# The transposes at the end of RWKV's pairs: from TensorE to 32x32 blocks that go by way of DRAM

## The chip, the core and the metric

The kernel runs on one core of a Trainium2 chip. The metric is the device time of one launch in microseconds (us). The core has five engines that run their own instruction streams in order and wait for each other through semaphores: PE (TensorE, matmuls; its weight loads are listed as PEld), DVE (VectorE), ACT (ScalarE), POOL (GpSimd) and SP (SyncE, which in this kernel issues nearly all DMAs). PE writes its results to PSUM banks; DVE and ACT take them from there.

## What is computed

One layer of a streaming encoder on 512 frames with 2048 channels, all float32. One input projection feeds two groups of heads, RWKV-7 (16 heads of 64 channels) and HGRN2 (8 heads of 128); their gated outputs go through one output projection, and a residual with LayerNorm ends the layer:

```
proj = x @ w_in
rw   = y + shift_mu * (y_prev - y)            # RWKV's columns: y is proj, y_prev one frame before
# RWKV-7, for each head, frame by frame:
S = S * w_t + (S @ a_t) b_t^T + v_t k_t^T;  o_t = S @ r_t
o = (o - mean) * rsqrt(var + GN_EPS) * gn_w + gn_b        # over the head's 64 channels
o_rwkv = (o + sum(r * k * r_k) * v) * silu(z)
o_hgrn = rms_norm(hgrn2(q, f, i)) * g_norm_w * silu(z_h)
out = layer_norm(ALPHA * x + concat(o_rwkv, o_hgrn) @ w_out) * ln_w + ln_b
```

The change is in the lines that begin with `o =` and `o_rwkv =`.

## The kernel before, in words

**Matmuls.** The projections run in a split form: each float32 operand is divided into a high part (rounded to the type `fp32r`) and a low part (the rest), and three matmuls add up high x high, high x low and low x high. All of them are issued in `three` (line 453). The input projection works through units of 128 columns, 16 k-tiles of 128 channels each; the order of the units (`_order`) is, for each group of two pairs of RWKV heads, k, r, v of both pairs, the z of the group before, then the HGRN columns. The last two units are z of pairs 6 and 7. The weights of a unit come in parts of 128x512; ACT writes the high part `wh` (line 337, called from `split`) and DVE the low part `wl` (line 347). `wh` and `wl` have three buffers each, and a part is asked for two parts ahead of its use. Weight loads (`wr`, line 430) are DMAs of 512 KB for two parts.

**RWKV.** Two heads make a pair (128 channels); there are 8 pairs in 4 groups of two. `rwkv_prep` forms the scan's operands and turns some of them by 32x32 blocks: `turned` has DVE transpose each 32x32 block of a tile (line 366), then 8 or 16 small DMAs on SP (line 401) bring the blocks to their places. `rwkv_group` inverts the triangular matrices, runs the scan over 8 chunks of 64 frames and adds the outputs. Up to here o has frames on the partitions: tile `S["o"]` is a view of `S["ot"]`, [128 frames, 4 blocks of frames, 128 channels].

**The end of a pair**, `rwkv_finish`: with frames on the partitions, it takes mean and variance over each head's 64 channels (DVE reductions, an ACT square, a power -0.5 on POOL) and scales o. Then o must have channels on the partitions, because z, the bonus `S["bv"]`, the weights gn_w and gn_b, and the output projection have them there. Four transposes on PE (line 328, the helper `tr`) bring it to a PSUM bank, and DVE gates it from there into tile `g`. All ends go through one queue, `finishes`: the end of pair 7 begins when that of pair 6 is done.

**The order of the work** is not found by hand. A planner (`Plan`) runs while the program is built, with a clock for each engine, a cost for each operation (`tt`, `stt`, `act`, `dtr`, `mm` and so on) and a due time for each tile (`plan.ready`, when it is there to be read; `plan.busy`, when its place may be written). The projections' matmuls are the main line; after each one `pump` goes through the queues of side threads in a fixed order (splits, evacuations, scans, groups, finishes, preps, heads, stores), and a thread's next operation is issued when by the plan's clocks its operands are nearly there: for DVE and ACT within 0.5 to 0.6 us of now, for PE 0.35 us after. A thread may also yield a condition (`room(...)`: so many free tiles of a kind; `by_now(t)`: t is there by the plan; `landed(...)`: the same and a free PSUM bank of the kind `mix`). The planner sets only the order of instructions in each engine's stream; on the chip they wait for semaphores.

**The output projection** has four blocks of 512 columns. The first (`rows` with d=0) takes the 16 gated tiles in the order 0 to 5, 8 to 13, 14, 6, 15, 7; 0 to 7 are RWKV's pairs, 8 to 15 HGRN's heads. At the start of k-tile j it calls `ahead`, which loads spilled tiles again and splits the gated tile j+1 into `xh` (ACT) and `xl` (DVE). At j = 8 it also asks for the LayerNorm's weights, `ln_wb`, one DMA of 2 MB on SP (line 1473). The tiles of all pairs but 6 and 7, and of all heads but the last two, are written to DRAM (`spill`) when they are done and read again here.

## Time and profile before

| | |
|---|---|
| time, median of 3 runs | 1050.75 us (1050.46 to 1051.28) |
| the profiled execution | 1050.24 us, of which the profile's span is 1048.5 |
| granted TensorE clock | 0.999 |
| PE busy | 1040.6 us, 99% of the span |
| DVE, ACT, POOL busy | 755.7, 437.6, 38.3 us |
| DMA | 114.79 MB in 87305 packets; SP's queue is busy for 36.6% of 16 engines' span |
| transposes on PE (line 328) | 88 of 128x128, of which 32 are RWKV's ends and 56 HGRN's |

Each timeline row has the start, the duration, the engine, the line, the operation with what it writes and reads, and in brackets the idle time before it with what ended it. Durations of matmuls overlap, so their price is read from start to start. A group's row gives busy time, the mean of one in ns, and the idle time before. The chain of waits is followed back from the last instruction; its pieces are a start, a length and what ran.

### The profile page before, as it was taken

The numbers are of one execution on the slowest core, as the hardware profiler recorded it, in microseconds if no ns is written. First come the engines' busy times: TensorE is split into PE (matmuls) and PEld (weight loads), VectorE is DVE, ScalarE is ACT, GpSimd is POOL, SyncE is SP. The second block draws the span as 40 slices with busy tenths as digits, with TensorE's granted clock in tenths as the row PEclk, the third lists the DMA queues.
The fourth block names the chain that finished last, engine by engine and source line by source line (L and its number), as shares of the span: only waits on it lengthen the run. The fifth ranks groups of instructions, "written<-read, shape, count | busy, mean of one in ns | idle before, by whom it ended". The sixth has DMA issues, their size and how long they took to land.

```text
span 1048.5 us, 18840 instructions
## 1 busy us (share of the span) xinstructions
PE 1040.6 (99%) x7342; PEld 865.1 (83%) x7342; DVE 755.7 (72%) x1653; ACT 437.6 (42%) x867; POOL 38.3 (4%) x81
## 2 busy tenths in 40 slices
PE   9999999999999999999999999999999999999997
PEld 8888888888888888888888888888888888888885
DVE  7465898667759987676689866865998778625556
ACT  6545333445353354452533353525334554323321
POOL 0000000000000000000000000000000002000000
PEclk9999999999999999999999999999999999999999
DMA  8134342222343522223534323234352244545613
GB/s 332 54 103 114 99 109 86 86 79 81 84 123 100 122 82 74 78 98 79 138 78 118 98 62 96 70 96 110 100 128 72 69 164 131 182 131 159 202 60 131
DMA packets 87305, 114.79 MB, mean 109 GB/s; under 512 B 56368, under 2 KB 58160, under 8 KB 87088
## 3 DMA queue, kind: packets, MB, share of 16 engines
q1 hardware_dynamic: 87072, 113.39, 36.6%
q8 instruction: 58, 0.95, 0.4%
q14 instruction: 31, 0.25, 0.1%
q10 hardware_dynamic: 144, 0.20, 0.1%
HBM read 99.92 MB, written 7.34 MB: 102 GB/s over the span
## 4 chain that ended last, share of the span: by engine, by line
PE 99%; DVE 1%; DVEq 0%; issue 0%
PE main L453 74%; PE mix L324 11%; PE mix L453 8%; PE main L1192 3%; PE main L324 2%; PE mix L328 1%; PE mix L1142 0%; DVE inv L356 0%; DVE inv L347 0%; DVE stats L1549 0%; DVEq L1663 0%; DVE mv L1357 0%; DVE bd L356 0%; DVE mv L352 0%; DVE inv L1140 0%
## 5 line engine op out<-in xcount | busy, mean ns | idle before, releaser
L453 PE MATMUL main<-xl,wh 128*128 128x512 f32 x864 | 341.1, 395 | 0.0
L453 PE MATMUL main<-xh,wl 128*128 128x512 f32 x864 | 341.1, 395 | 0.0
L453 PE MATMUL main<-xh,wh 128*128 128x512 f32 x864 | 340.9, 395 | 0.0
L337 ACT ACTIVATE wh<-wr 128x512 fp32r<-128x512 f32 x299 | 186.9, 627 | 237.1 <-PE main L453 180.5
L347 DVE TENSOR_TENSOR wl<-wr,wh 128x512 fp32r<-128x512 f32 x299 | 203.8, 682 | 61.8 <-ACT wh L337 60.1
L453 PEld LDWEIGHTS main<-xh,wh 128*128 128x128 f32 x864 | 162.4, 188 | 33.0
L453 PEld LDWEIGHTS main<-xh,wl 128*128 128x128 f32 x864 | 162.5, 188 | 32.6
L453 PEld LDWEIGHTS main<-xl,wh 128*128 128x128 f32 x864 | 162.4, 188 | 32.6
L453 PE MATMUL main<-wl,xh 128*128 128x512 f32 (+1 forms) x262 | 102.6, 392 | 0.0
L453 PE MATMUL main<-wh,xh 128*128 128x512 f32 (+1 forms) x262 | 102.1, 390 | 0.0
L453 PE MATMUL main<-wh,xl 128*128 128x512 f32 (+1 forms) x262 | 101.6, 388 | 0.0
L453 PEld LDWEIGHTS main<-wh,xh 128*128 128x128 f32 x262 | 49.2, 188 | 9.9
L453 PEld LDWEIGHTS main<-wh,xl 128*128 128x128 f32 x262 | 49.2, 188 | 9.7
L453 PEld LDWEIGHTS main<-wl,xh 128*128 128x128 f32 x262 | 49.2, 188 | 9.6
L338 ACT ACTIVATE t<-main,om 128x512 f32<-128x512 f32 x33 | 22.4, 687 | 51.1 <-PE main L453 41.6
L356 DVE SCALAR_TENSOR_TENSOR t<-main,pr,t 128x511 f32<-128x511 f32 x33 | 24.4, 747 | 26.5 <-ACT t L338 26.2
L347 DVE TENSOR_TENSOR inv<-inv,inv 64x30 f32<-64x30 f32 (+14 forms) x120 | 38.6, 322 | 2.9
L347 DVE TENSOR_TENSOR inv<-inv 64x30 f32<-64x30 f32 (+14 forms) x120 | 38.4, 320 | 2.3
L347 DVE TENSOR_TENSOR t<-t,tot 128x256 f32<-128x256 f32 x96 | 37.8, 414 | 1.8 <-PE mix L324 1.7
L356 DVE SCALAR_TENSOR_TENSOR bd<-mix,pc,bd 64x64 f32<-64x64 f32 x112 | 31.7, 283 | 7.5 <-PE mix L324 5.2
L337 ACT ACTIVATE zz<-mix 64x64 f32<-64x64 f32 x63 | 13.8, 220 | 46.9 <-PE mix L324 45.8
L338 ACT ACTIVATE t<-main 128x512 f32<-128x512 f32 x32 | 18.5, 598 | 30.7 <-PE main L453 30.2
(222 smaller groups left out, 1328.0 us busy)
## 6 DMA issues: line engine op xcount, KB each, us to landing
wr<-w_all SPq DMA_DIRECT2D x156, 512.0 KB, 3.6
q<-head SPq DMA_DIRECT2D x15, 448.0 KB, 5.9
q<-q SPq DMA_DIRECT2D x128, 32.0 KB, 2.4
g<-x_r SPq DMA_DIRECT2D x16, 256.0 KB, 3.8
spill<-g SPq DMA_DIRECT2D x12, 256.0 KB, 2.7
out<-q SPq DMA_DIRECT2D x12, 256.0 KB, 2.4
t<-spill SPq DMA_DIRECT2D x10, 256.0 KB, 4.2
zz<-ksq SPq DMA_DIRECT2D x64, 32.0 KB, 2.6
```

Of the source, the lines that this page charges most:

```text
L324: return Op([("pe", cost, lambda: pe.matmul(o, l, r, start=start, stop=stop, **kw))], [l, r], [o], mode="narrow" if narrow else "main" if ...
L328: return Op([("pe", 0.11, lambda: pe.transpose(o, i, ident))], [i], [o])
L337: return "act", cost, lambda: sc_e.activation(o, i, f, scale=scale)
L338: return "act", cost, lambda: sc_e.activation(o, i, f, scale=scale, bias=bias)
L347: return dve_op([a, b], o, lambda: dve.tensor_tensor(o, a, b, f), base=0.16 if o.shape[0] < P and size(o) == C and o.tensor.name in tags e ...
L356: return dve_op([a, b], o, lambda: dve.scalar_tensor_tensor(o, a, s, b, f1, f2), per=0.00113, base=0.085 if o.shape[0] == P else 0.25 if s ...
L453: pe.matmul(ps, l, r, start=first and i == 0, stop=last and i == 2)
L1192: pe.matmul(pss[a], *ops, start=k == 0 and low == of == 0, stop=k == KT - 1 and low == 1)
```

## The change

The four PE transposes of a pair's end are replaced by a way through DVE and DRAM. `turned_far` has DVE transpose the 32x32 blocks of o into tile `g`, used here as a temporary. One DMA writes it to a tile `far` in DRAM (256 KB, rows of 2 KB); after 4.4 us of the plan's PE clock, four DMAs read it back with the blocks in exchanged places (64 KB each, in pieces of 512 bytes) into `S["ot"]`, the tile that o was in. It is due 4.7 us later. ACT then applies the scale gn_w and the shift gn_b (both halved, as before) and puts the frames in order on the way into `g`; DVE adds `bv` and multiplies by z's gate. Before, two operations of DVE did this, the first out of PSUM. A `ksq` tile for the gate is now taken after the turn, not before.

The two pairs of a group get a queue each, so their ends run beside each other. And `turned` now marks its temporary tile as busy until its DMAs have landed by the plan.

```diff
@@ turned, and new functions
-        plan.ready[name] = (plan.clock["pe"] + 3.0, "dma")
+        plan.ready[name] = plan.busy[tmp.tensor.name] = (plan.clock["pe"] + 3.0, "dma")
+
+    def turned_far(dst, src, tmp):
+        yield dtr(tmp, src.rearrange("p c (b f) -> p b c f", f=32))
+        yield lambda: by_now(tmp)
+        far = dpool.tile([4, 32, 4, T // 4], F32, tag=nm("far"), name=nm("far"))
+        nc.sync.dma_start(far.rearrange("a p b r -> (a p) b r"), tmp.rearrange("p b c f -> p b (c f)"))
+        at = plan.clock["pe"] + 4.4
+        yield lambda: plan.clock["pe"] >= at
+        for b in range(4):
+            nc.sync.dma_start(dst[32 * b : 32 * b + 32].rearrange("p a c f -> p a (c f)"),
+                              far[:, :, b].rearrange("a p r -> p a r"))
+        plan.ready[dst.tensor.name] = plan.busy[dst.tensor.name] = (plan.clock["pe"] + 4.7, "dma")
+
+    def in_blocks(t):
+        return t.rearrange("p (c a f) -> p c a f", a=4, f=32)
+
+    def blocks(t):
+        return t.rearrange("p (a c f) -> p a c f", c=4, f=32)
@@ rwkv_finish
         yield has(S, "z", "bv")
-        yield room(g=1, ksq=1)
+        yield room(g=1)
         g = take("g")
+        yield from turned_far(blocks(S["ot"]), o_all, blocks(g))
+        yield room(ksq=1)
         sz = take("ksq")
         z = S["z"]
-        yield landed(o_all)
-        po = take("mix")
-        for j in range(4):
-            yield tr(po[:, j * P : j * P + P], o_all[:, j])
         yield act(sz, z, AF.Tanh, scale=0.5)
-        yield stt(g, po, hcol(HGW, p), S["bv"], ALU.mult, ALU.add)
-        drop(po)
+        yield act(in_blocks(g), blocks(S["ot"]).rearrange("p a c f -> p c a f"), AF.Identity,
+                  scale=hcol(HGW, p), bias=hcol(HGB, p))
         yield stt(z, sz, 1.0, z, ALU.add, ALU.mult)
-        yield stt(g, g, hcol(HGB, p), z, ALU.add, ALU.mult)
+        yield tt(g, g, S["bv"], ALU.add)
+        yield tt(g, g, z)
@@ rwkv_group
-                plan.add(finishes, rwkv_finish(S, 2 * grp + i))
+                plan.add(finishes[i], rwkv_finish(S, 2 * grp + i))
@@ queues
-    groups, finishes, preps = plan.queue(), plan.queue(), plan.queue()
+    groups, finishes, preps = plan.queue(), [plan.queue(), plan.queue()], plan.queue()
```

## The prediction

> **What bounds the kernel now.** I read the page first: busy shares, then the chain that ended last.

> ```profile
> span 1048.5 us, 18840 instructions
> PE 1040.6 (99%) x7342; PEld 865.1 (83%) x7342; DVE 755.7 (72%) x1653; ACT 437.6 (42%) x867; POOL 38.3 (4%) x81
> ...
> PE 99%; DVE 1%; DVEq 0%; issue 0%
> ```

> TensorE is never without work for long. Its own waits, the whole list:

> ```profile
> PE mix L324 <- ACT ksq L1409: 1.5, 1, 1.5
> PE mix L1142 <- DVE inv L1140: 1.1, 1, 1.1
> PE mix L324 <- DVE bd L356: 0.4, 1, 0.4
> ```

> These are 3.0 us in all, so each microsecond of PE work taken out shortens the run, and each new PE wait lengthens it. The place to look is the junction at the end: the ends of pairs 6 and 7 run beside the first column block of the output projection, which consumes `gated[6]` as its 14th and `gated[7]` as its 16th k-tile. The chain there, from 868 to 910 us, and the PE timeline around pair 7's transposes:

> ```profile
> 880.39 0.44 PE mix L328 x4
> 880.83 7.99 PE main L453 x35
> 888.82 0.44 PE mix L328 x4
> 889.25 4.12 PE main L453 x18
> 893.37 0.44 PE mix L328 x4
> 893.81 13.43 PE main L453 x59
> ```

> ```profile
> 892.98 0.39 PE L453 MATMUL main<-wh,xh 128*128 128x512 f32 x1
> 893.21 0.60 PE L328 MATMUL mix<-cst,t 128*128 128x128 f32 x4
> 893.56 0.48 PE L453 MATMUL main<-wl,xh 128*128 128x512 f32 x1
> 893.88 0.40 PE L453 MATMUL main<-wh,xl 128*128 128x512 f32 x1
> ```

> A plain matmul takes 13.43/59 = 0.228 us. From 892.98 to 893.88 two of them pass, 0.455 us; 0.90 are used, so four transposes with both turns cost 0.445 us, as the chain's 0.44 says. The sets at 880.39 and 893.37 are pairs 6 and 7; 888.82 is an HGRN head and stays. The 60 matmuls from 893.56 to 907.2 are five k-tiles of 12, so I number the block's k-tiles 0 to 15: tile 11 starts at 893.56 and a tile is 2.73 us.

> **The change: what is gained.** Eight pairs give up four transposes each: 8 x 0.445 = 3.6 us of PE, 0.34% of the run. Nothing else of PE changes, and a `mix` bank is free earlier, which no PE wait above asks for.

> [...]

> **What is added on DVE and ACT.** The nearest rows, by group:

> ```profile
> L366 DVE STREAM_TRANSPOSE ksq<-t 128x512 f32<-128x512 f32 x8 | 5.6, 701 | 0.0
> L356 DVE SCALAR_TENSOR_TENSOR g<-mix,half,t 128x512 f32<-128x512 f32 x16 | 12.0, 747 | 9.0 <-PE mix L328 8.8
> L356 DVE SCALAR_TENSOR_TENSOR g<-g,half,t 128x512 f32<-128x512 f32 x8 | 6.0, 746 | 0.1
> L347 DVE TENSOR_TENSOR t<-t,sm 128x512 f32<-128x512 f32 x16 | 11.1, 692 | 4.7 <-POOL sm L379 4.4
> L338 ACT ACTIVATE t<-main,om 128x512 f32<-128x512 f32 x33 | 22.4, 687 | 51.1 <-PE main L453 41.6 <-PE main L1192 8.6 <-DVE xl L347 0.8
> ```

> Per pair DVE gains a block transpose (0.70) and two tensor_tensors (1.38) and loses two scalar_tensor_tensors (1.49): +0.6 us, 4.7 us over eight pairs on an engine with 293 us free. ACT gains one scaled pass, 0.69 us, 5.5 in all with 611 free. Both hide under PE as throughput; if not, they would cost at most 10.2 us, and I take nothing, because splits run two parts ahead of PE. The same ACT row shows projections evacuated as soon as PE ends them (41.6 of 51.1 us idle are waits for PE): the `t` tiles that pairs now hold some 10 us longer have room in groups 0 to 2, and no one there needs `gated` before the spill. There I cost the longer chain at nothing; a shortage could cost up to those 10 us, a lucky order gain 1. Marking `tmp` busy until its DMAs land moves only planned starts: 0, within 1 us either way.

> **DMAs.** Each pair issues one 256 KB write and four 64 KB reads on SP: 40 issues, 4 MB. The prices:

> ```profile
> spill<-g SPq DMA_DIRECT2D x12, 256.0 KB, 2.7
> ...
> zz<-ksq SPq DMA_DIRECT2D x64, 32.0 KB, 2.6
> ...
> big<-ln_wb SPq DMA_DIRECT2D x1, 2048.0 KB, 10.1
> ```

> A write of 2.7 fits in the 4.4 us left for it, and reads near 2.6 (four issues: some 4) in the 4.7. So the plan's path is 0.7 + 0.6 + 4.4 + 4.7 = 10.4 us up to ACT, against about 1 us now. In groups 0 to 2 it holds. At the junction it meets the last row: 2 MB of `ln_wb`.

> **The junction, step by step** (times of before; the 24 earlier transposes move everything alike). DVE, POOL and SP there:

> ```profile
> 878.83 0.69 DVE L347 TENSOR_TENSOR t<-t,sm 128x512 f32<-128x512 f32 x1
> ...
> 884.59 0.68 DVE L360 TENSOR_REDUCE sm<-t 128x8 f32<-128x512 f32 x1
> ```

> ```profile
> 877.15 1.64 POOL L379 TENSOR_TENSOR sm<-sm,mhalf 128x8 f32<-128x8 f32 x1 [9.47 <-DVE sm L353]
> ```

> ```profile
> 885.13 1.26 SPq L1473 DMA_DIRECT2D big<-ln_wb  x1
> 890.09 0.33 SPq L430 DMA_DIRECT2D wr<-w_all  x1
> ```

> Pair 6's last norm multiply ends at 879.5. Pair 7 waits for its turn until 884.59 now; with its own thread it starts with pair 6, on a DVE already nearly full there. That can move pair 6 by -0.6 to +1.2 (one foreign instruction ahead, or two); I take +0.5: 880.0. POOL does the second power behind the first, so pair 7 is ready some 1.6 to 2 us later, 881.8. Pair 6: block transpose to 880.7, write at 881.4 (the planner lets about 0.6 pass, as between 879.5 and PE's transposes), reads in SP's order at 885.8. `ln_wb` is asked for at the start of tile 8, now 885.13 - 0.45 = 884.7, **ahead of them**. Does a later DMA overtake it? The next weight load was issued at 890.09; ACT's timeline:

> ```profile
> 890.50 0.63 ACT L337 ACTIVATE wh<-wr 128x512 fp32r<-128x512 f32 x1 [1.60 <-PE main L453]
> 891.04 0.62 ACT L337 ACTIVATE xh<-g 128x512 fp32r<-128x512 f32 x1
> ...
> 893.18 0.63 ACT L337 ACTIVATE wh<-wr 128x512 fp32r<-128x512 f32 x1 [1.00 <-PE main L453]
> 893.72 0.61 ACT L337 ACTIVATE xh<-g 128x512 fp32r<-128x512 f32 x1
> 896.54 0.63 ACT L337 ACTIVATE wh<-wr 128x512 fp32r<-128x512 f32 x1 [2.21 <-DMA wr<-w_all]
> ```

> It landed at about 896.4, 6.3 us after its issue and 1.2 after `ln_wb` (885.13 + 10.1 = 895.2): it queued. [...]

> So pair 6's reads land 0.6 (half the load's bytes) to 1.2 us (small packets) after 894.8: 895.4 to 896.0, where the plan has 890.5; pair 7's 0.6 to 1.2 later. The new ACT pass stands in ACT's order from about 890.0 of the plan, pair 7's from about 891.8, and ACT is in order: behind it queue the weight split of tile 12 (now at 890.50), the gated split of tile 12 (891.04), and on DVE the low halves, behind the pair's two tensor_tensors. Released at 895.7, ACT does the pass (0.55 at its rate), then the splits: 896.9 and 897.4, DVE's low halves at 898.2 and 898.8. PE's tile 12 is due at 893.56 + 2.73 - 0.89 = 895.4 and can run its third matmul from 898.8, so it starts 2.9 us late. If pair 7's pass is ahead of the splits too, 3.9. If tile 11's split (due one tile earlier) is caught, tile 11 waits from 892.7 to 897.1: 4.4. Bounds 2.9 to 4.4, and I take the middle, 3.6. After that PE runs a tile late, and `gated[6]` (about 897.7) and `gated[7]` come in time.

> **Sum.** On the profiled execution (1050.24 us, span 1048.5 and 1.7 around it): -3.6 + 3.6 = 0, 1050.2. The median of the runs is 0.5 above it: 1050.7; own range 1050.0 to 1051.6.

> **Rivals.** *The wait is escaped.* If both passes come into ACT's order behind tile 12's splits (plan time past 892.7, 2.7 us later than I think), only tile 13's `gated[6]` is late: pass 896.3, tensor_tensors 897.6, splits 898.9 and 899.5 against a need at 898.1: 1.0 us, hence 1050.7 - 3.6 + 1.0 = 1048.1. If the reads get ahead of `ln_wb` (both norms 1 to 3 us earlier) nothing waits: 1047.1. For: 1 us on pair 6 decides, planned orders shift by that. Against: two threads on one DVE and one POOL make it later, and pair 7 needs it as well.

> *Pair 7's write is caught too*, the slower side: if its norm ends after 884.7 - 0.6 - 0.7 = 883.4, the write queues behind `ln_wb`, SP holds the reads (and weight loads behind them) until about 896, they land 2.6 later at 898.6, pass 899.2, two tensor_tensors, splits done at 901.6: tile 12 runs from 901.2, 5.8 late: 1050.7 - 3.6 + 5.8 = 1052.9. For: POOL's row, 1.64 us a piece, and DVE's load. Against: my 881.8 leaves 1.6 us.

> **Chances.** This kernel's measurement tells 0.2%, 2.1 us, from no change: faster is under 1048.65, slower over 1052.85. The forecast 0.53, escape 0.30, the second trip 0.17. Range 1047.0 (nothing waits) to 1053.3 (the second trip with tile 11 caught), less than 2 in 10 outside.

> **What would show it.** The 32 RWKV transposes gone and PE busy down by 3.6; `ln_wb` ahead of the last reads on SP; reads there landing after 8 us or more, elsewhere under 4.7; an ACT idle of 5 us ending in a DMA of the pair's tile near 895; a PE wait of 3 to 4 us on ACT or DVE splits. No PE wait there and 1047 would make the forecast wrong; so would waits of PE in groups 0 to 2.

## The result, and the profile after

The changed kernel takes 1067.59 us (median of 4 runs, 1066.48 to 1069.47) against 1050.61 for the one before, timed beside it: a ratio of 1.0163, 95% interval 1.0145 to 1.0181. The prediction was 1050.7 with a range of 1047.0 to 1053.3, so the time lies far outside of it.

The page of the changed kernel (its lines are those of the new file: `three` is now line 474, weight loads are 451, the turned blocks' small DMAs still 401, the write to `far` 413, the four reads 417):

```profile
span 1065.8 us, 18884 instructions
PE 1044.9 (98%) x7310; PEld 866.0 (81%) x7310; DVE 757.8 (71%) x1660; ACT 442.6 (42%) x876; POOL 38.6 (4%) x81
...
PE 90%; SPq 3%; DMA 2%; DVE 2%; issue 1%; ACT 1%; DVEq 0%; ACTq 0%
```

PE has 32 instructions less, as it should. But it is busy 4.3 us longer, and idle 1065.8 - 1044.9 = 20.9 us against 7.9. The chain of waits, 99% PE before, is 90% PE now; most of the rest is SP's queue, DMAs and DVE. PE's own waits in the changed kernel (total, times, longest):

```profile
PE main L474 <- ACT xh L337: 4.5, 2, 3.9
PE mix L324 <- ACT ksq L337: 3.6, 2, 2.1
PE mix L324 <- DVE ksq L347: 2.9, 3, 1.0
PE mix L324 <- DVE uph L347: 1.9, 1, 1.9
```

Two more, of 1.5 and 1.1 us, are at the ends of the run and were there before; one of 0.6 us has no releaser. The first row here is at the last junction (912 to 921 us), which the prediction had looked at. The other three are 8.4 us in groups 0 to 2 (near 298, 516 to 524 and 727 us), where it had expected nothing.

**Group 0, step by step.** SP's timeline of the changed kernel (start, length of the issues, what):

```profile
279.74 5.16 SPq L401 DMA_DIRECT2D q<-q  x8
285.00 0.54 SPq L413 DMA_DIRECT2D far<-g  x1
285.59 2.56 SPq L401 DMA_DIRECT2D q<-q  x4
288.25 0.54 SPq L451 DMA_DIRECT2D wr<-w_all  x1
288.83 3.29 SPq L401 DMA_DIRECT2D q<-q  x4
292.22 1.97 SPq L417 DMA_DIRECT2D t<-far  x4
```

DVE had the blocks turned at 280.7 (its row starts at 280.02 and takes 0.71), but SP was busy with `turned`'s small DMAs of the next group's preparation, 0.64 us an issue, and wrote `far` only at 285.0. Another eight of them and a weight load stand between the write and the reads. The reads go out from 292.2 to 294.2. Now ACT, and then PE:

```profile
295.78 0.81 ACT L338 ACTIVATE g<-t,half 128x512 f32<-128x512 f32 x1 [7.27 <-DMA t<-far]
296.50 0.61 ACT L337 ACTIVATE wh<-wr 128x512 fp32r<-128x512 f32 x1
297.02 0.61 ACT L337 ACTIVATE ksq<-t 128x512 fp32r<-128x512 f32 x1
```

```profile
297.69 0.50 PE L324 MATMUL mix<-ksq,ones_r 128*128 128x512 f32 x1 [2.14 <-ACT ksq L337]
299.18 0.51 PE L324 MATMUL mix<-ksq,ones_r 128*128 128x512 f32 x1 [0.99 <-DVE ksq L347]
...
300.22 0.63 PE L474 MATMUL main<-xh,wl 128*128 128x512 f32 x1
300.65 0.63 PE L474 MATMUL main<-xh,wh 128*128 128x512 f32 x1
...
303.41 0.40 PE L474 MATMUL main<-xl,wh 128*128 128x512 f32 x1
303.65 0.40 PE L474 MATMUL main<-xh,wl 128*128 128x512 f32 x1
```

ACT stands 7.27 us at the new pass, with a weight split and the operand `ksq` of another thread behind it. PE then waits for that `ksq`, 2.14 us, and for its low half from DVE, 0.99. After the wait PE's matmuls follow each other every 0.43 us, not 0.23 (300.22 to 300.65 against 303.41 to 303.65), for 3.4 us; the profile gives the granted clock as 0.50 there and 1.00 before and after. So waits of 3.13 us are followed by a loss of an estimated 1.7 us (half of 3.4), about half as much again. In groups 1 and 2 ACT stands at the same pass, 5.00 us (until 512.79) and 6.80 us (until 725.15).

**The last junction.** SP again:

```profile
895.21 0.38 SPq L1493 DMA_DIRECT2D big<-ln_wb  x1
895.65 0.42 SPq L413 DMA_DIRECT2D far<-g  x1
900.27 0.33 SPq L451 DMA_DIRECT2D wr<-w_all  x1
905.39 1.98 SPq L417 DMA_DIRECT2D t<-far  x4
907.42 0.52 SPq L413 DMA_DIRECT2D far<-g  x1
```

Pair 6's write, not only its reads, is behind `ln_wb`; SP can issue the reads only when it has landed, 9.7 us later, and pair 7's write stands behind those reads. ACT reaches the pass at 901.3, runs it at 909.13, and PE waits 3.91 us at 912.64:

```profile
909.13 0.81 ACT L338 ACTIVATE g<-t,half 128x512 f32<-128x512 f32 x1 [7.85 <-DMA t<-far]
```

```profile
912.64 0.79 PE L474 MATMUL main<-wh,xh 128*128 128x512 f32 x1 [3.91 <-ACT xh L337]
```

### The profile page after: what moved, and what is told of

Same layout as the page of the kernel before. It is cut to its first block, busy times and chain, and to the rows that moved or that the text cites. A ratio compares the mean times of both kernels' runs of the same rounds, so it can differ in the third digit from the quotient of the medians.

```text
span 1065.8 us, 18884 instructions
## 1 busy us (share of the span) xinstructions
PE 1044.9 (98%) x7310; PEld 866.0 (81%) x7310; DVE 757.8 (71%) x1660; ACT 442.6 (42%) x876; POOL 38.6 (4%) x81
## 4 chain that ended last, share of the span: by engine, by line
PE 90%; SPq 3%; DMA 2%; DVE 2%; issue 1%; ACT 1%; DVEq 0%; ACTq 0%
PE main L474 66%; PE mix L324 10%; PE mix L474 8%; PE main L1212 3%; SPq L401 2%; PE main L324 2%; DMA far<-g 1%; DMA t<-far 1%; PE mix L328 1%; DMA zz<-ksq 1%; SPq L417 1%; DVE g L347 0%; DVE wl L347 0%; PE mix L1162 0%; ACT g L338 0%
## 5 line engine op out<-in xcount | busy, mean ns | idle before, releaser
L337 ACT ACTIVATE wh<-wr 128x512 fp32r<-128x512 f32 x299 | 185.8, 626 | 220.4 <-PE main L474 150.4
L347 DVE TENSOR_TENSOR wl<-wr,wh 128x512 fp32r<-128x512 f32 x299 | 203.5, 682 | 74.2 <-ACT wh L337 73.0
L338 ACT ACTIVATE t<-main,om 128x512 f32<-128x512 f32 x33 | 22.3, 685 | 50.9 <-PE main L474 41.6
L356 DVE SCALAR_TENSOR_TENSOR t<-main,pr,t 128x511 f32<-128x511 f32 x33 | 24.4, 746 | 24.8 <-ACT t L338 24.8
L347 DVE TENSOR_TENSOR inv<-inv,inv 64x30 f32<-64x30 f32 (+14 forms) x120 | 38.5, 321 | 2.5
L347 DVE TENSOR_TENSOR inv<-inv 64x30 f32<-64x30 f32 (+14 forms) x120 | 38.4, 320 | 2.4
L356 DVE SCALAR_TENSOR_TENSOR bd<-mix,pc,bd 64x64 f32<-64x64 f32 x112 | 31.7, 283 | 11.5 <-PE mix L324 9.3
L347 DVE TENSOR_TENSOR t<-t,tot 128x256 f32<-128x256 f32 x96 | 37.5, 415 | 2.0 <-PE mix L324 1.5
L338 ACT ACTIVATE t<-main 128x512 f32<-128x512 f32 x32 | 18.5, 595 | 33.4 <-PE main L474 33.2
L337 ACT ACTIVATE zz<-mix 64x64 f32<-64x64 f32 x64 | 14.0, 219 | 40.2 <-PE mix L324 39.6
## 6 DMA issues: line engine op xcount, KB each, us to landing
g<-x_r SPq DMA_DIRECT2D x16, 256.0 KB, 4.2
spill<-g SPq DMA_DIRECT2D x12, 256.0 KB, 2.1
out<-q SPq DMA_DIRECT2D x12, 256.0 KB, 2.4
t<-spill SPq DMA_DIRECT2D x10, 256.0 KB, 4.1
```

The costliest lines, as they stand in the source:

```text
L337: return "act", cost, lambda: sc_e.activation(o, i, f, scale=scale)
L338: return "act", cost, lambda: sc_e.activation(o, i, f, scale=scale, bias=bias)
L347: return dve_op([a, b], o, lambda: dve.tensor_tensor(o, a, b, f), base=0.16 if o.shape[0] < P and size(o) == C and o.tensor.name in tags e ...
L356: return dve_op([a, b], o, lambda: dve.scalar_tensor_tensor(o, a, s, b, f1, f2), per=0.00113, base=0.085 if o.shape[0] == P else 0.25 if s ...
```

## The experiments

All ratios are to the kernel before, timed on the same chip beside each run.

| run | edit | median us | ratio (95%) |
|---|---|---|---|
| after | the change | 1067.59 | 1.0163 (1.0145 to 1.0181) |
| e1 | threads and busy mark alone | 1051.23 | 1.0006 (0.9997 to 1.0016) |
| e2 | due after 12.0 | 1058.46 | 1.0078 (1.0063 to 1.0093) |
| e3 | `ln_wb` in block 2 | 1068.35 | 1.0171 (1.0136 to 1.0206) |
| e4 | e2 + e3 | 1059.32 | 1.0086 (1.0069 to 1.0102) |
| e5 | DMAs on ACT's queue | 1054.03 | 1.0031 (1.0020 to 1.0042) |
| e6 | e2 + gate's tile late | 1053.72 | 1.0033 (1.0020 to 1.0047) |
| e7 | e6, pairs 6 and 7 on PE | 1048.99 | 0.9986 (0.9976 to 0.9995) |
| e8 | e5 + gate's tile late | 1060.76 | 1.0096 (1.0080 to 1.0113) |
| e9 | after, pairs 6 and 7 on PE | 1059.12 | 1.0081 (1.0066 to 1.0096) |
| e10 | e6 + `ln_wb` in block 2 | 1051.95 | 1.0014 (1.0005 to 1.0023) |
| e11 | e8 + `ln_wb` in block 2 | 1061.31 | 1.0097 (1.0082 to 1.0112) |
| e12 | e8 + e9 | 1050.74 | 1.0002 (0.9992 to 1.0011) |
| e13 | e6 + `ln_wb` at k-tile 14 | 1049.39 | 0.9987 (0.9978 to 0.9996) |

### The small edits alone (e1)

The kernel before, with a queue for each pair's end and with `plan.busy[tmp]`; the transposes stay on PE.

```diff
-        plan.ready[name] = (plan.clock["pe"] + 3.0, "dma")
+        plan.ready[name] = plan.busy[tmp.tensor.name] = (plan.clock["pe"] + 3.0, "dma")
-                plan.add(finishes, rwkv_finish(S, 2 * grp + i))
+                plan.add(finishes[i], rwkv_finish(S, 2 * grp + i))
```

> The kernel before with only the two small edits: a queue for each pair's end, and the temporary tile of the turned blocks marked busy until its DMAs land. The transposes stay on TensorE. Theory A (the loss comes from ACT passes that stand in ACT's order before their data can have landed): 1049 to 1052 us, no PE waits beyond the 3.0 us of before, since no pass waits for a DMA. Theory B (the new order of the ends, or the busy mark, crowds DVE and ACT and by itself makes PE wait): 1056 us or more, with PE waits for DVE or ACT at the groups' ends.

1051.23 us against 1050.67 beside it, no change that can be told. PE's waits, complete:

```profile
PE mix L324 <- ACT ksq L1409: 1.5, 1, 1.5
PE mix L1142 <- DVE inv L1140: 1.1, 1, 1.1
PE mix L324 <- DVE t L347: 0.2, 1, 0.2
```

By themselves the threads and the mark cost nothing that can be told; theory B falls.

### The due time (e2), ln_wb (e3), and both (e4)

```diff
-        plan.ready[dst.tensor.name] = plan.busy[dst.tensor.name] = (plan.clock["pe"] + 4.7, "dma")
+        plan.ready[dst.tensor.name] = plan.busy[dst.tensor.name] = (plan.clock["pe"] + 12.0, "dma")
```

> The changed kernel with one number altered: the turned tile is due 12.0 us after its reads are issued by the plan, not 4.7, so ACT's pass comes later in ACT's order and the same data has longer to land. Theory A: the PE waits at the ends of groups 0 to 2 (8.3 us idle and the slow matmuls after them) go away; at the last junction the pass is no longer early, but gated[6] comes later by 7 us, so a PE wait of 3 us or more stays there. 1055 to 1062 us. Theory B: the same waits stay, 1066 to 1069 us.

> The changed kernel with the 2 MB load of ln_wb asked for at the start of the second column block of the output projection, not at k-tile 8 of the first. Theory A: the waits at the last junction (4.5 us idle and the slow matmuls after them) shrink to under 1.5 us, those of groups 0 to 2 stay: 1059 to 1063 us. If the junction's wait comes from DVE's load or from the late scan and not from the queue behind ln_wb, 1066 to 1069 us and a wait of 4 us stays there.

> The changed kernel with both edits of the two runs before it: due after 12.0 us, and ln_wb in the second block. Theory A: no PE wait at groups 0 to 2; the junction waits for gated[6], which is due 7 us later but without the queue: 0 to 4 us. 1047 to 1053 us. Theory B: 1062 us or more.

e2 takes 1058.46 us, 9.1 less than the change. But for the one at the end of the run, no wait of PE for `ksq` or `uph` is left in it; at the junction a large one stays:

```profile
PE main L474 <- ACT xh L337: 4.3, 1, 4.3
```

In group 0 the reads go out at 291.69 us, hardly sooner than the 292.22 of the changed kernel, but ACT's pass now runs at 297.92 without a wait. So the due time was the cause in groups 0 to 2: a later place in ACT's order takes the waits away though the data comes no sooner. e3 missed its theory A. With `ln_wb` out of the way the junction was no better (waits of 2.8 and 2.4 us), and the time is in the range of the other branch, the late scan or DVE's load; its four executions lie far apart (1064.16 to 1073.28). e4 equals e2 and misses its 1047 to 1053: 3.3 us of wait for `xh` and 1.7 for a weight split stay. SP and ACT in e3:

```profile
895.96 0.42 SPq L413 DMA_DIRECT2D far<-g  x1
901.06 0.33 SPq L451 DMA_DIRECT2D wr<-w_all  x1
901.44 1.85 SPq L417 DMA_DIRECT2D t<-far  x4
```

```profile
908.43 0.81 ACT L338 ACTIVATE g<-t,half 128x512 f32<-128x512 f32 x1 [6.36 <-DMA t<-far]
```

Even without the 2 MB the reads land seven microseconds after the first of them is issued, behind a 512 KB weight load, and the write is as late as before. Something else makes the pair's end late.

### Another queue (e5)

```diff
-        nc.sync.dma_start(far.rearrange("a p b r -> (a p) b r"), tmp.rearrange("p b c f -> p b (c f)"))
+        nc.scalar.dma_start(far.rearrange("a p b r -> (a p) b r"), tmp.rearrange("p b c f -> p b (c f)"))
...
-            nc.sync.dma_start(dst[32 * b : 32 * b + 32].rearrange("p a c f -> p a (c f)"),
+            nc.scalar.dma_start(dst[32 * b : 32 * b + 32].rearrange("p a c f -> p a (c f)"),
```

> The changed kernel with the write to far and the four reads issued on ACT's DMA queue, not on SP's; due times as in the changed kernel (4.4 and 4.7 us). Theory A1 (the data comes late because its DMAs stand in SP's order behind other threads' small DMAs at 0.65 us each, and at the last junction behind ln_wb in SP's queue): the reads land in time, PE waits at groups 0 to 2 fall from 8.3 us to under 2, the junction's from 4.5 to under 2: 1048 to 1054 us, with some 0.5 us of ACT for each issue. Theory A2 (the way through DRAM itself takes longer than 9 us whatever the queue): the waits stay, 1064 us or more.

1054.03 us with the due times of the change. The eight executions spread from 1051.08 to 1055.44, and the trace is that of the shortest, whose mean granted clock is 1.000; the five longer ones (1053.99 and more) had a lower one, 0.997 to 0.998 against 0.999 to 1.000. So the trace shows the queue's effect, but not what lengthens the median by 3 us. In group 0:

```profile
280.56 0.34 ACTq L413 DMA_DIRECT2D far<-g  x1
...
285.33 0.83 ACTq L417 DMA_DIRECT2D t<-far  x2
...
289.31 0.82 ACT L338 ACTIVATE g<-t,half 128x512 f32<-128x512 f32 x1 [0.66 <-DMA t<-far]
```

The write goes out as soon as DVE is done, the first reads 4.8 us later, and ACT waits 0.66 us where it waited 7.27. The way through DRAM is as short as the prediction had it; SP's order made it long. PE's waits in groups 0 to 2 fall from 8.4 to 1.7 us, the junction's from 4.5 to 1.0. This run also prices the change on PE: the same 7310 instructions as the changed kernel, and the page says

```profile
PE 1037.6 (99%) x7310; PEld 861.7 (82%) x7310; DVE 758.6 (72%) x1660; ACT 443.6 (42%) x876; POOL 38.6 (4%) x81
```

1037.6 against 1040.6 before: 3.0 us gained, of 3.6 predicted. (Busy time is a rough price: e10 and e13, with the same matmuls, have 1038.3, a gain of 2.3.) And 1044.9 against 1037.6: the changed kernel's PE loses 7.3 us while it is busy, to the slow stretches after its waits above all.

### The held tile (e6), and the last pairs on PE (e7, e9)

```diff
-        yield room(ksq=1)
-        sz = take("ksq")
         z = S["z"]
-        yield act(sz, z, AF.Tanh, scale=0.5)
         yield act(in_blocks(g), blocks(S["ot"]).rearrange("p a c f -> p c a f"), AF.Identity,
                   scale=hcol(HGW, p), bias=hcol(HGB, p))
-        yield stt(z, sz, 1.0, z, ALU.add, ALU.mult)
+        yield room(ksq=1)
+        sz = take("ksq")
+        yield act(sz, z, AF.Tanh, scale=0.5)
         yield tt(g, g, S["bv"], ALU.add)
+        yield stt(z, sz, 1.0, z, ALU.add, ALU.mult)
```

> The changed kernel with the due time of 12.0 us, and the gate's ksq tile (one of two) taken after ACT's pass and not held while the data travels. Theory C (a held ksq tile stops the next group's preparation, so its scan ends late by PE's clock and the last junction waits): the last group's first reduction comes 4 to 7 us earlier than at 879.0 us as with the due time alone, the junction's PE wait of 4.3 us shrinks below 1.5 us: 1048 to 1053 us. Without C: the scan ends where it did, and the time stays at 1057 to 1060 us.

1053.72 us, 4.7 less than e2. Of the two `ksq` tiles one was held while the data travelled, and the next group's preparation needs both (`room(ksq=2)`). The start of the last group's scan shows it (POOL clears `rt`): first before, then e2, then e6.

```profile
753.27 0.20 POOL L382 MEMSET rt<- 64x128 f32 x1
```

```profile
760.28 0.20 POOL L382 MEMSET rt<- 64x128 f32 x1
```

```profile
754.36 0.20 POOL L382 MEMSET rt<- 64x128 f32 x1
```

Seven microseconds late with the tile held, one without; the first reduction of pair 6 comes at 873.6 and not 879.0. Theory C holds for the scan. Its second half missed: the junction still waits, 3.6 us, and the time lies just outside of 1048 to 1053. There SP shows what the prediction had described:

```profile
882.47 0.38 SPq L1493 DMA_DIRECT2D big<-ln_wb  x1
882.97 0.35 SPq L413 DMA_DIRECT2D far<-g  x1
886.16 0.33 SPq L451 DMA_DIRECT2D wr<-w_all  x1
892.26 2.10 SPq L417 DMA_DIRECT2D t<-far  x4
```

e7 is e6 with an `if p < 6` around the new end; pairs 6 and 7 keep the old one. e9 is the same branch in the changed kernel, with nothing else altered.

> As the run before it, with pairs 6 and 7 turned by TensorE as in the kernel before; six pairs go by way of DRAM. If PE's saved transposes are worth what the prediction says, 6 x 0.445 = 2.7 us less than before, and no PE wait: 1047.5 to 1049 us. If the extra DMAs or DVE work cost something that no PE wait shows, 1050 us or more.

> The changed kernel, due times and gate as changed, with pairs 6 and 7 alone turned by TensorE as before. Theory A: the junction's waits go (4.5 us idle, and the slow matmuls after them, some 3 us), those of groups 0 to 2 stay: 1059 to 1062 us. If the groups' waits only shift work that the junction would have waited for anyway, 1064 us or more.

e7 takes 1048.99 us, 0.14% faster than before, and the gain of 2.7 us is there but for one PE wait of 1.4 us that it has near 815 us (below). e9 takes 1059.12, as its theory A had it: the junction alone is worth 1067.6 - 1059.1 = 8.5 us, the groups before it 1059.1 - 1050.5 = 8.6, both net of the transposes saved.

### ln_wb once more (e10, e13)

e10 adds e3's edit to e6; e13 asks for it in the first block, at k-tile 14, behind both pairs' reads:

```diff
-            if j == 8:
+            if j == 14:
```

> All pairs by way of DRAM on SP, due after 12.0 us, the gate's ksq tile taken after ACT's pass, and ln_wb asked for in the second column block. In the run without the last edit, far's write for pair 6 was issued 0.5 us behind ln_wb and its reads 9.3 us after it. If that queue is what is left of the loss, the reads follow the write within 5 us, the junction's PE wait of 4.0 us falls below 1.0, and the time is 1047.5 to 1050 us. If the pair's end is late by its own length, a wait of 3 us or more stays: 1052 us or more.

> All pairs by way of DRAM on SP, due after 12.0 us, the gate's ksq tile late, and ln_wb asked for at k-tile 14 of the first column block: behind both pairs' reads, but some 6 us earlier than in the run that asked in the second block, where DVE met it too early (PE waited 1.5 us for a weight split behind it). If that is what was left, PE waits beyond before's are under 1 us (without the one for nothing that the profile shows, near 815 us) and the time is 1047 to 1049.5 us, the 3.6 us of the prediction less that wait. If the way through DRAM is too long for pair 6 by itself, a PE wait of 1 us or more for an xh split stays and the time is 1050 us or more.

In e10 the reads follow the write after 4.2 us (883.42 and 887.58), and the junction waits 0.4 us instead of 4.0. But 1051.95 us, which misses 1047.5 to 1050: DVE now meets `ln_wb` before it has landed (the transfer is 1% of the chain that ended last), with a weight split behind it, and PE waits 1.5 us for that. e13 removes it; of its waits of PE, these two are not those at the ends of the run:

```profile
PE mix L324 <- issue: 1.8, 1, 1.8
PE main L474 <- ACT xh L337: 0.7, 1, 0.7
```

1049.39 us, 0.13% faster than before, with all eight pairs by way of DRAM on SP. (The trace is that of the longest of its eleven executions, 1050.39.) So the change needed three more edits to be worth something: a due time that SP can hold, the gate's tile taken late, and `ln_wb` out of the pairs' way.

### ACT's queue with the late tile (e8, e11, e12)

e8 is e5 with e6's late tile (due after 4.7), e11 adds e3's edit, e12 keeps pairs 6 and 7 on PE.

> All pairs by way of DRAM on ACT's DMA queue, due after 4.7 us as in the changed kernel, the gate's ksq tile taken after ACT's pass; ln_wb where it was. If the held ksq tile costs the run on ACT's queue its PE wait of 1.7 us for a ksq operand and part of the scan's lateness, it gains 2 to 3 us on that run: 1050 to 1052.5 us. If only the queue mattered, it stays at 1053 to 1055 us.

> As the run before it, with ln_wb in the second column block. If the two queues share the DMA engines so that ln_wb slows the reads at the junction, it gains another 1 to 2 us: 1048 to 1050.5 us; otherwise it equals that run within 1 us.

> Six pairs by way of DRAM on ACT's queue, due after 4.7 us, the gate's ksq tile late, pairs 6 and 7 by TensorE. If six pairs' transposes, 2.7 us, are the gain and nothing waits: 1047.5 to 1049 us. If issuing five DMAs a pair from ACT, about 0.5 us each, makes the weights' splits late: 1050 us or more.

e8 missed both of its ranges. e11 equals e8 within 1 us, and e12 is over 1050, as their second branches had it, but not for the reasons given there. e8 is 6.7 us slower than e5, with waits of 3.8 and 3.0 us at the junction. Its write stands on ACT's queue 0.2 us behind `ln_wb` on SP's (883.10), where e5's was 1.0 us ahead, and the reads wait for it:

```profile
883.30 0.34 ACTq L413 DMA_DIRECT2D far<-g  x1
...
892.12 1.77 ACTq L417 DMA_DIRECT2D t<-far  x4
```

The reads follow the write after 8.8 us. In e11, without `ln_wb` there, they follow after 5.6 (883.01 and 888.63), and in e5 after 3.3: `ln_wb` is worth 3.2 us of it, and here another queue was no way around the 2 MB. In both e8 and e11 a 512 KB weight load went out on SP 0.6 us ahead of the write, in e5 0.6 us behind it; whether that makes the other 2.3 us was not tested. And here ACT itself stands at the read, with the splits behind it (4.75 us in e8, 1.53 in e11). In e11 PE waits 4.2 us for DVE's part of an HGRN head and 2.6 for a weight split behind `ln_wb`; why the head is late there was not settled. e12, 1050.74, equals before: without the junction, ACT's queue gives back what PE gains. Its trace has waits of 1.7 us for `ksq`, and eight matmuls 0.43 us apart, 3.4 us in all, from 605.96; its mean granted clock is 0.998, against 0.999 to 1.000 in the other nine executions.

## Why the prediction was wrong

**The gain.** 3.6 us predicted, 2.3 to 3.0 measured on PE with the same matmuls (e10, e13, e5); e7 and e13 end 1.3 to 1.5 us below before. Right in kind.

**"A write of 2.7 fits in the 4.4 us ... In groups 0 to 2 it holds."** This step failed. The transfers are that short (medians of 2.3 us for the write and 2.0 for a read in the changed kernel, and 8.8 us for e5's whole way up to ACT's pass), but SP's issues go out one behind the other (the write 4.3 us after the blocks were turned), and at that place the next group's `turned` puts 16 DMAs of some 0.65 us into it; the planner spaces them by 0.4 us. The rows are in the trace of before, at a place that the prediction does not look at:

```profile
275.06 5.17 SPq L401 DMA_DIRECT2D q<-q  x8
280.33 0.55 SPq L430 DMA_DIRECT2D wr<-w_all  x1
280.92 5.18 SPq L401 DMA_DIRECT2D q<-q  x8
```

I costed the added issues of groups 0 to 2 by what they move and not by what they stand behind. Measured: 15 us from the turned blocks to ACT's pass, not the 9 to 10 of the plan.

**"Both hide under PE as throughput."** Busy time was near (ACT +5.0 us of 5.5, DVE +2.1 of 4.7), the conclusion not. In group 0 the late operand held not only the one pass but ACT for 7.3 us, with the weight split and `ksq` behind it. The reason given, weight splits two parts ahead of PE, held: PE's list has no wait for `wh` or `wl`. But other threads' operands, `ksq` and `uph`, stand in the same order with no such lead, and PE waits for them. I had used this mechanism at the junction and did not ask for it elsewhere.

**"The `t` tiles ... have room."** The scarce tile was another, `ksq`, with two places. The edit moves its `take` to a point from which it is held until the data arrives; that put the last scan 7 us late (e2 against before; in the changed kernel `rt` is cleared at 767.29, 14 us late, PE's waits of groups 0 to 2 included), and e6 took 4.7 us off e2. It was not a term of the sum.

**The junction.** The mechanism was found, `ln_wb` ahead of the pair's data in the queue and ACT's splits behind the pass, and e6 against e10 confirms it (4.0 us of wait against 0.4). The rival of the second trip was nearer than the forecast: pair 6's write, not only pair 7's, was caught. The late scan is one reason. The other is that the 24 earlier transposes do not "move everything alike": in e6, whose scan is 1 us late, `ln_wb` is issued at 882.47 us and not at 885.13, while pair 6's first reduction comes at 873.62 against 872.67 before, its block transpose at 881.93 against the 880.0 forecast, and its write 0.5 us behind `ln_wb`. e3 shows that in the changed kernel itself it was not the only cause. The wait was put at 3.6 us and is 4.5; that the size came so near, though the write was caught and not the reads alone, is partly luck.

**The price of a wait.** I counted idle time alone. On the profiled execution: idle +13.0, PE's work -3.0 (e5), work slowed down +7.3 (what is left): +17.3 us of span. The profile's clock records give half clock for 3.41 us from 299.70, 3.41 from 729.78 and 6.83 from 910.69. PE is busy for 11.7 of these 13.7 us and loses half of that, an estimated 5.8 us; the other 1.5 are not traced to a row. Ahead of the first of these stretches stand waits of 2.14 and 0.99 us.

## What to carry to other kernels

On SP and ACT, where what stood behind a late instruction waited with it (7.27 us on ACT in group 0), a due time is a promise for everything behind it: when a planner puts an instruction that waits for a DMA into a stream, the due time must include what stands in the issuing queue, read from that queue's timeline at each place where it will happen. Where a compute step is exchanged for a round trip, ask which scarce buffers are now held for its length. Near the end of a tight chain, keep the short way and move only what has slack: here six pairs of eight (e7) gave all the gain that eight gave (e13).

## What the runs showed that I had not expected

A DMA of 32 rows by 8 pieces of 128 bytes holds SP 0.61 us (median; 0.65 from one to the next), a 512 KB weight load 0.33. And every kernel with the way through DRAM on SP has a PE wait of 0.6 to 1.8 us between 815 and 829 us for nothing that the profile shows, as does e5 (1.2 us at 817); before, e1, e8, e11 and e12 have none there. In e7 and e13, 1.4 and 1.8 us, it is about as large as the gain that is left. Its cause is open.
